# Decode attention: the rotary cache gathered with its features on the partitions, and the tied order of four transposes

## The chip, the cores and the metric

The kernel runs on one core of one Trainium2 chip. The metric is the device time of one execution in microseconds. The engines work side by side, each in the order of its own queue: PE (matrix products; its weight loads are shown as PEld), DVE (vector operations), ACT (scalar functions and copies), POOL (here it issues the gathers) and SP (here it issues the other loads and stores). A DMA queue moves data between the chip's memory (HBM) and the on-chip memory of 128 partitions.

## The reference, cut to what matters

One step of one layer: a feed-forward block, a mixer (a gated recurrence and a latent attention side by side), and a second feed-forward block, for a prompt of 512 tokens and 8 decoded sequences of 4 tokens each. The change is in the latent attention of the decoded sequences. Their past is 4096 tokens each, held in pages of 128 tokens that a page table names; a past token has a latent row of 256 numbers and a rotary row of 64:

```python
past_c = cache_kv_latent[l][page_table].reshape(Bs, past_len, KV_LORA)
past_r = cache_k_rope[l][page_table].reshape(Bs, past_len, QK_ROPE)
...
s = (jnp.einsum('bqhr,bsr->bhqs', ql, c_kv) + jnp.einsum('bqhd,bsd->bhqs', qr, k_rope)).astype(jnp.float32) * scale
s = jnp.where(k_pos[None, None, None, :] <= qp[None, None, :, None], s, -jnp.inf)
p = jax.nn.softmax(s, axis=-1).astype(c_kv.dtype)
return jnp.einsum('bhqs,bsr->bqhr', p, c_kv)
```

So a score is a sum over 256 + 64 features, and the value is taken from the latent rows alone. All in 32-bit floats.

## The kernel before, in words

The phases follow one another: first feed-forward block, mixer of the prompt, and then the decode (`decode`, L1437), which shares its time with the second feed-forward block of the prompt's first half (the generator `gb`). The loop at L1517 calls them in turn: a step of the decode, then about one step of the feed-forward block, of which there are 100 while the decode has 94.

The decode works on 16 halves: 8 sequences, 2048 past tokens at a time (`Half`, L1352). A half is two blocks of 1024 tokens. For a block POOL gathers the latent rows by an indirect DMA (`gather`, L1360: 128 partitions x 8 tokens x 256 features, 1 MB, into one of seven slots) and the rotary rows by another (`gather_r`, L1369: tile `rraw`, 128 x 8 x 64, 256 KB, two buffers). Both come with tokens on the partitions. A matmul needs the features there, so DVE turns the blocks by transposing squares of 32 x 32 (`turn`, L1376, the transposes of L1381): five stages per half, one of 64 features each, two transposes of 128 x 512 per stage. Stage 0 is the rotary one (`JS` = (8, 9) at L65), stages 1 to 4 the latent ones. The result of a stage is a tile `kh`, of which there are four buffers.

For scores (`score`, L1384) PE multiplies each stage with a query laid out in blocks of 64 x 32, eight small matmuls at a time for each of the two 32-feature groups; the products of all five stages add up in one bank. Then (end of `score`) ACT and DVE copy the scores out and DVE takes a row maximum (`self.top`, L1401). In `peak` (L1403) PE spreads the maximum, DVE reduces it (L1407) and takes the masked sum that serves as bias (L1410), ACT takes the exponential (L1411), DVE transposes the probabilities (L1413), and DVE and ACT place them into `pbuf` (L1417; four of the sixteen copies are DVE's). In `value` (L1419) PE multiplies them with the latent rows.

The halves are staggered. The outer loop counts n, with five steps st each. In an iteration half n-2 is scored (stages 0 to 2 at st 2, stages 3 and 4 at st 4, by `RUNS` at L68), half n-3 has its `peak` at st 1 and its values at st 4, after which its latent slots are gathered into again, and one stage is turned per step, in order of a list `ups`: at st 2 the last stage of half n-2, at st 3 and 4 stages 0 and 1 of half n-1, and at st 0 and 1 of the next iteration its stages 2 and 3. The rotary rows of a half are gathered as soon as the rotary stage of the half before has been turned.

Within an engine the order is not simply the order of the text: a planner lists the instructions by the text's order and its own reckoning of when each is ready, so a later one that is ready sooner may go first. `tc.issue_after(x)` ties what is traced under it behind x in the queue of x's engine; it adds no wait for x's end. Before the change one turn per iteration is tied, the one at st 4, behind `self.top`.

Of the kernel before, what the change touches and what calls it, by code (L numbers as in the profile page):

```python
# [73 lines left out]
C_W = C_SH + 2 * TS  # L74
# [4 lines left out]
def _constants():  # L79
    cf = np.zeros((P, C_W), np.float32)  # L80
    p = np.arange(P)
    cf[:, C_ID : C_ID + P] = np.eye(P, dtype=np.float32)
    pos = np.concatenate([np.arange(TP), PAST + np.tile(np.arange(NT), NB)]).astype(np.float32)
    half = RD // 2
    inv = np.power(np.float32(10000.0), -np.arange(half, dtype=np.float32) / np.float32(half)).astype(np.float32)
    ang = pos[None, :] * inv[p % half][:, None]
    cf[:, C_COS : C_COS + T] = np.cos(ang)
    cf[:, C_SIN : C_SIN + T] = np.sin(ang) * np.where(p % RD < half, -1.0, 1.0)[:, None]
    t = np.arange(T)
    cf[:, C_RST : C_RST + T] = np.where(t < TP, t % CH != 0, t % NT != 0)[None, :]  # L90
# [8 lines left out]
    cf[:, C_P8] = p % 16  # L99
    cf[:, C_S4 : C_S4 + 32] = p[:, None] % 32 == np.arange(32)[None, :]  # L100
# [10 lines left out]
def hybrid_step_kernel(  # L111
    ctx: ExitStack,
    tc: tile.TileContext,
    x_t, pool_c, pool_r, state, ptl, vecs, w_g, w_u, w_d, w_in, w_kr, w_q, w_qr, w_kv, w_uk, w_o, cf, cm,
# [656 lines left out]
    q2 = qsT.rearrange("p j b t h -> p j (b t h)")  # L771

# [16 lines left out]
    with scope("mix") as mx_:  # L789
# [293 lines left out]
        with scope("at2"):  # L1083
# [154 lines left out]
            def decode_prep():  # L1238
                for j in range(10):
# [62 lines left out]
    with scope("dec"):  # L1302
# [49 lines left out]
        class Half:  # L1352
            def __init__(self, n):
# [4 lines left out]
                self.craw, self.rraw, self.kh = [], [], []  # L1358
# [10 lines left out]
            def gather_r(self):  # L1369
                for blk in (2 * self.n, 2 * self.n + 1):  # L1370
                    rraw = mk([P, ROWS, RD], F32, "rraw", 2)
                    off = bass.IndirectOffsetOnAxis(ap=idx[:, blk : blk + 1], axis=0)
                    nc.gpsimd.indirect_dma_start(rraw.rearrange("p a r -> p (a r)"), None, pool_r, off)
# [10 lines left out]
            def score(self, st):  # L1384
# [3 lines left out]
                for jj, j in enumerate(JS[st]):  # L1388
                    for c in range(4):
                        for r in range(2):  # L1390
                            rs = slice(r * 64, r * 64 + 64)
                            kh = self.kh[st][rs, c // 2, c % 2 * 4 : c % 2 * 4 + 4, jj]
                            nc.tensor.matmul(self.s[r][c * 32 : c * 32 + 32, :P], q[rs, j], kh, start=st + jj == 0, stop=st == len(JS) - 1 and jj == 1, skip_group_check=True)  # L1393
# [9 lines left out]
            def peak(self):  # L1403
# [6 lines left out]
                nc.vector.scalar_tensor_tensor(mq, m, -SCALE, selL, op0=ALU.mult, op1=ALU.mult, accum_out=mb)  # L1410
# [3 lines left out]
                for c in range(4):  # L1414
                    for g in range(4):
                        src = pt[c * 32 : c * 32 + 32, g // 2 * 4 : g // 2 * 4 + 4, g % 2 * 16 : g % 2 * 16 + 16]
                        (nc.scalar.copy if g else nc.vector.tensor_copy)(self.p[g * 32 : g * 32 + 32, c // 2, c % 2 * 4 : c % 2 * 4 + 4, self.i * 16 : self.i * 16 + 16], src)  # L1417
# [19 lines left out]
        def decode():  # L1437
            H = [Half(n) for n in range(NH2)]
            blocks = [h_ for h_ in H for _ in range(2)]
            ups = [(h_, st) for h_ in H for st in range(len(JS))]  # L1440
# [6 lines left out]
            def turn(top):  # L1447
                if ups:
                    h_, st = ups.pop(0)
                    with tc.issue_after(top.ins) if top is not None else nullcontext():  # L1450
                        h_.turn(st)
                    if st == 0 and h_.n + 1 < NH2:
                        H[h_.n + 1].gather_r()

            for n in range(NH2 + 4):
# [4 lines left out]
                for st in range(len(JS)):  # L1460
                    if at(2):
                        for k in RUNS.get(st, ()):
                            at(2).score(k)
# [204 lines left out]
def _arrays(inputs):  # L1668
# [41 lines left out]
```

## Time and profile before

| | |
|---|---|
| time, median of 3 runs | 1250.94 us (1250.69 to 1252.57) |
| profiled execution, span from first to last instruction | 1241.4 us |
| what lies around the span, if the profiled execution was like the median (its own time is not given beyond the span) | 9.5 us |
| busy share of the span: PE, PEld, DVE, ACT, POOL | 98%, 93%, 79%, 60%, 6% |
| granted TensorE clock, mean | 0.999 |
| HBM traffic over the span | 156 GB/s |

The span is from the first to the last instruction of the program, the time includes what lies around it. An engine's busy time is the union of its instructions. Matmuls overlap, and their ends are modelled, so a busy PE is not PE at its peak. In a row of a timeline stand the start and the duration in microseconds, engine, line, operation, the tiles written and read, the shape, the count of merged instructions, and in brackets how long the engine had been idle and what ended that. In a row of waits stands who waited on whose result, in total, how many times, and the longest. Buffer numbers are left out of names, and a slot that several tiles use shows under one name (`q` is a large slot that also holds queries, scores and latent rows).

### The profile page before, as it was taken

The page shows a single profiled execution, that of the slowest core. Times are in us where ns is not written, and L with a number is a line of the kernel's source. Part 1 is how long each engine was busy: PE and PEld are TensorE (multiplying, and loading weights), DVE is VectorE, ACT ScalarE, POOL GpSimd, SP SyncE. Part 2 cuts the span into 40 slices and gives each one's busy share as a digit, 9 for nine tenths or more (in the row PEclk, how much of TensorE's full clock was granted, in tenths as well). Part 3 has the DMA queues.
Part 4 walks back from the last instruction along what each step waited for, and adds up shares of the span by engine and source line. Part 5 has one row for each costly group of instructions (what it writes and reads, how often), then busy time and mean ns, then how long its engine had stood idle before and what let it go on. Part 6 is the DMA issues. An engine that isn't in the chain of part 4 may idle for free.

```text
span 1241.4 us, 29997 instructions
## 1 busy us (share of the span) xinstructions
PE 1215.0 (98%) x12366; PEld 1151.3 (93%) x12366; DVE 982.7 (79%) x1976; ACT 738.8 (60%) x1559; POOL 76.5 (6%) x80
## 2 busy tenths in 40 slices
PE   8999999999999999999999999999999999999997
PEld 6999999999999989988898888888888999999997
DVE  7897788878678888786877899999998778566665
ACT  7675545455366744545758766666656776554455
POOL 0000000000000000000001312322310000000000
PEclk9999999999999999999999999999999999999999
DMA  6232333232264213333233868878776635545451
GB/s 238 86 115 90 103 103 102 86 99 91 62 221 147 82 54 105 88 94 130 85 105 117 339 214 303 310 282 323 258 275 232 198 106 188 184 137 188 150 151 60
DMA packets 73113, 195.59 MB, mean 158 GB/s; under 512 B 12336, under 2 KB 27728, under 8 KB 68240
## 3 DMA queue, kind: packets, MB, share of 16 engines
q1 hardware_dynamic: 64512, 150.47, 37.3%
q0 software_dynamic: 7168, 41.95, 9.2%
q8 instruction: 97, 1.59, 0.5%
q10 hardware_dynamic: 1296, 1.26, 0.3%
q14 instruction: 40, 0.33, 0.1%
HBM read 183.97 MB, written 9.67 MB: 156 GB/s over the span
## 4 chain that ended last, share of the span: by engine, by line
PE 79%; DVE 11%; ACT 7%; issue 2%; DMA 2%; SPq 0%; DVEq 0%; ACTq 0%
PE acc L259 29%; PE acc L277 13%; PE dn L259 8%; PE Y L575 7%; PE X L575 4%; PE Z L575 4%; DVE kh L1381 3%; PE acc L731 3%; DVE wl L251 2%; ACT wh L250 1%; PE s L1393 1%; ACT pbuf L1417 1%; DMA wraw<-w_g 1%; PE pa L952 1%; PE o L1426 1%
## 5 line engine op out<-in xcount | busy, mean ns | idle before, releaser
L250 ACT CAST wh<-wraw 128x1024 fp32r<-128x1024 f32 (+2 forms) x194 | 185.0, 957 | 164.3 <-PE acc L259 103.7
L251 DVE TENSOR_TENSOR wl<-wraw,wh 128x1024 fp32r<-128x1024 f32 (+2 forms) x194 | 214.6, 1108 | 72.2 <-ACT wh L250 71.6
L277 PE MATMUL acc<-uha,wh 128*128 128x256 f32 (+1 forms) x528 | 155.5, 295 | 0.1
L277 PE MATMUL acc<-uha,wl 128*128 128x256 f32 (+1 forms) x528 | 150.0, 285 | 0.8 <-DVE wl L251 0.7
L277 PE MATMUL acc<-ula,wh 128*128 128x256 f32 (+1 forms) x528 | 150.5, 286 | 0.0
L259 PE MATMUL acc<-uhb,wh 128*128 128x288 f32 (+1 forms) x432 | 128.0, 296 | 0.0
L259 PE MATMUL acc<-uhb,wl 128*128 128x288 f32 (+1 forms) x432 | 127.0, 295 | 1.0 <-DVE wl L251 0.8
L259 PE MATMUL acc<-ulb,wh 128*128 128x288 f32 (+1 forms) x432 | 127.5, 295 | 0.0
L277 PEld LDWEIGHTS acc<-uha,wh 128*128 128x128 f32 x528 | 99.2, 188 | 8.8 <-issue 7.9
L277 PEld LDWEIGHTS acc<-uha,wl 128*128 128x128 f32 x528 | 99.2, 188 | 2.3 <-DVE wl L251 1.6
L277 PEld LDWEIGHTS acc<-ula,wh 128*128 128x128 f32 x528 | 99.4, 188 | 1.6 <-issue 1.2
L259 PEld LDWEIGHTS acc<-uhb,wl 128*128 128x128 f32 x432 | 81.2, 188 | 1.6 <-DVE wl L251 1.6
L259 PEld LDWEIGHTS acc<-uhb,wh 128*128 128x128 f32 x432 | 81.0, 187 | 0.2 <-ACT uhb L170 0.2
L259 PEld LDWEIGHTS acc<-ulb,wh 128*128 128x128 f32 x432 | 81.1, 188 | 0.1
L259 PE MATMUL dn<-hh,dh 128*128 128x272 f32 x256 | 74.3, 290 | 0.0
L259 PE MATMUL dn<-hh,dl 128*128 128x272 f32 x256 | 73.7, 288 | 0.0
L259 PE MATMUL dn<-hl,dh 128*128 128x272 f32 x256 | 73.6, 288 | 0.0
L277 PE MATMUL acc<-uhb,wh 128*128 128x272 f32 x176 | 52.8, 300 | 0.0
L1417 ACT COPY pbuf<-pt 32x64 f32<-32x64 f32 x192 | 46.5, 242 | 10.1 <-DVE pt L1413 7.3
L259 PE MATMUL acc<-hlb,wh 128*128 128x288 f32 x176 | 52.1, 298 | 0.0
L259 PE MATMUL acc<-hhb,wh 128*128 128x288 f32 x176 | 51.8, 298 | 0.0
L1393 PE MATMUL s<-kh,q 64*32 64x128 f32 x2560 | 48.0, 273 | 3.5 <-DVE kh L1381 3.5
(632 smaller groups left out, 3881.3 us busy)
## 6 DMA issues: line engine op xcount, KB each, us to landing
wraw<-w_u SPq DMA_DIRECT2D x66, 512.0 KB, 4.3
wraw<-w_g SPq DMA_DIRECT2D x65, 512.0 KB, 3.9
wraw<-w_d SPq DMA_DIRECT2D x40, 384.0 KB, 3.5
wraw<-w_in SPq DMA_DIRECT2D x24, 512.0 KB, 3.5
wraw<-w_d SPq DMA_DIRECT2D x32, 320.0 KB, 3.1
wraw<-w_d SPq DMA_DIRECT2D x16, 512.0 KB, 3.8
wraw<-w_o SPq DMA_DIRECT2D x16, 512.0 KB, 3.7
g_S<-state SPq DMA_DIRECT2D x4, 512.0 KB, 4.4
```

What stands on the lines that cost most here:

```text
L250: nc.scalar.copy(wh[:, :kt], w[:, :kt])
L251: nc.vector.tensor_tensor(wl[:, :kt], w[:, :kt], f32(wh[:, :kt]), op=ALU.subtract)
L259: nc.tensor.matmul(out, a, b, start=n == 0, stop=n == last)
L277: nc.tensor.matmul(acc[:, :n], a[:, k], b[:, k], start=k + i == 0, stop=k == kt - 1 and i == 2)
L575: nc.tensor.matmul(bank, a[p][:, k], b[q][:, k], start=first and k + n == 0, stop=k == 3 and n == 2, skip_group_check=True)
L731: nc.tensor.matmul(accs[x, d], wts[d][p][:, k], hs[k // 2][q][:, k % 2, x], start=k + n == 0, stop=k == nf - 1 and n == 2)
L952: nc.tensor.matmul(po[es, c].rearrange("p (n m) -> p n m", m=m), kx[:, cs], up(qx[:, cs], m), start=True, stop=True, skip_group_check=True)
L1381: nc.vector.transpose(kh[:, g].rearrange("p a j k -> p a (j k)"), src)
L1393: nc.tensor.matmul(self.s[r][c * 32 : c * 32 + 32, :P], q[rs, j], kh, start=st + jj == 0, stop=st == len(JS) - 1 and jj == 1, skip_group_c ...
L1417: (nc.scalar.copy if g else nc.vector.tensor_copy)(self.p[g * 32 : g * 32 + 32, c // 2, c % 2 * 4 : c % 2 * 4 + 4, self.i * 16 : self.i * ...
L1426: nc.tensor.matmul(o[g : g + 32, :R], self.p[:, c, a], self.craw[c][:, a], start=i + c == 0 and a < 4, stop=i + c == 2 and a >= 4, skip_gr ...
```

## The change

The rotary cache is laid out differently on the host, before the kernel starts: within a page first the number of a feature in its group of 32, then the group (two), then a token's place among eight, then sixteen. A gathered row is now 1 KB and holds one feature of each group for all 128 tokens of a page; before it was 2 KB and held 64 features of eight tokens. A second index (`idr`, 64 columns instead of 32), made in `decode_prep` from a page table of its own, names these rows, and `gather_r` makes four gathers of 128 KB per half into tiles `rk` instead of two of 256 KB into `rraw`. They arrive with features on the partitions: the rotary stage needs no transposes any more, and PE reads `rk` directly.

The rotary gathers of a half are issued at st 3, when the half before has had its rotary stage scored. The four remaining stages are turned at other steps: stages 1 and 2 of half n-1 at st 3 and st 4, stages 3 and 4 of half n-2 at st 1, one tied behind the masked sum of `peak`, the other behind DVE's last placed copy. The order of the scores is as before, with the rotary stage first.

```diff
             def decode_prep():
+                pr_sb = mk([P, 2 * NBLK], I32, "pr_sb")
+                nc.sync.dma_start(pr_sb, ptr)
+                p32 = mk([P, 1], F32, "p32")
+                nc.sync.dma_start(p32, cf[:, C_P32 : C_P32 + 1])
+                nc.vector.tensor_scalar(out=idr, in0=pr_sb, scalar1=float(RD // 2), scalar2=p32, op0=ALU.mult, op1=ALU.add)
...
             def gather_r(self):
                 for blk in (2 * self.n, 2 * self.n + 1):
-                    rraw = mk([P, ROWS, RD], F32, "rraw", 2)
-                    off = bass.IndirectOffsetOnAxis(ap=idx[:, blk : blk + 1], axis=0)
-                    nc.gpsimd.indirect_dma_start(rraw.rearrange("p a r -> p (a r)"), None, pool_r, off)
-                    self.rraw.append(rraw)
+                    rk = mk([P, 2, 2, ROWS, 16], F32, "rk", 2)
+                    for i in range(2):
+                        off = bass.IndirectOffsetOnAxis(ap=idr[:, 2 * blk + i : 2 * blk + i + 1], axis=0)
+                        nc.gpsimd.indirect_dma_start(rk[:, i].rearrange("p j a k -> p (j a k)"), None, pool_r, off)
+                    self.rk.append(rk)
...
-                    src = self.craw[g][:, :, j * 32 : j * 32 + 64] if j < 8 else self.rraw[g]
+                    src = self.craw[g][:, :, j * 32 : j * 32 + 64]
...
-                            rs = slice(r * 64, r * 64 + 64)
-                            kh = self.kh[st][rs, c // 2, c % 2 * 4 : c % 2 * 4 + 4, jj]
-                            nc.tensor.matmul(self.s[r][c * 32 : c * 32 + 32, :P], q[rs, j], kh, start=st + jj == 0, stop=st == len(JS) - 1 and jj == 1, skip_group_check=True)
+                            rs, as_ = slice(r * 64, r * 64 + 64), slice(c % 2 * 4, c % 2 * 4 + 4)
+                            out = self.s[r][c * 32 : c * 32 + 32, :P]
+                            if j < 8:
+                                kh = self.kh[st - 1][rs, c // 2, as_, jj]
+                            else:
+                                kh = self.rk[c // 2][rs, :, jj, as_].rearrange("p i a k -> p a i k")
+                                out = out.rearrange("p (a i k) -> p a i k", a=4, i=2)
+                            nc.tensor.matmul(out, q[rs, j], kh, start=st + jj == 0, stop=st == len(JS) - 1 and jj == 1, skip_group_check=True)
...
-                nc.vector.scalar_tensor_tensor(mq, m, -SCALE, selL, op0=ALU.mult, op1=ALU.mult, accum_out=mb)
+                self.spread = nc.vector.scalar_tensor_tensor(mq, m, -SCALE, selL, op0=ALU.mult, op1=ALU.mult, accum_out=mb)
...
+                        if g == 0:
+                            self.placed = put
...
-            ups = [(h_, st) for h_ in H for st in range(len(JS))]
+            ups = [(h_, st) for h_ in H for st in range(1, len(JS))]
...
-            def turn(top):
+            def turn(after=None):
                 if ups:
                     h_, st = ups.pop(0)
-                    with tc.issue_after(top.ins) if top is not None else nullcontext():
+                    with tc.issue_after(after.ins) if after is not None else nullcontext():
                         h_.turn(st)
-                    if st == 0 and h_.n + 1 < NH2:
-                        H[h_.n + 1].gather_r()
...
-                        if n == 0:
-                            H[0].gather_r()
                         gather(2 + n // 2)
+                    if st == 3 and at(1):
+                        at(1).gather_r()
...
-                    if n > 1 or n == 1 and st >= 1:
-                        if n != 2 or st >= 2:
-                            turn(at(2).top if at(2) and st == len(JS) - 1 else None)
+                    if n > 0 and st > 2:
+                        turn(at(2).top if at(2) and st == len(JS) - 1 else None)
+                    if n > 1 and st == 1:
+                        turn(at(3) and at(3).spread)
+                        turn(at(3) and at(3).placed)
...
-        "pool_r": g["cache_k_rope"].reshape(-1, ROWS * RD),
+        "pool_r": np.ascontiguousarray(g["cache_k_rope"].reshape(-1, 16, ROWS, 2, 32).transpose(0, 4, 3, 2, 1)).reshape(-1, 16 * ROWS * 2),
+        "ptr": np.ascontiguousarray(np.repeat(g["page_table"].reshape(NBLK, 4, 2), 32, axis=1).transpose(1, 0, 2)).reshape(P, 2 * NBLK),
```

More of the change, by code (lines that the diff above doesn't have):

```diff
@@ L73 @@
 C_SH = C_SL + 16
-C_W = C_SH + 2 * TS
+C_P32 = C_SH + 2 * TS
+C_W = C_P32 + 1
 V_QG, V_KVG, V_HGG, V_LB = 48, 54, 56, 57
@@ L113, in hybrid_step_kernel @@
     tc: tile.TileContext,
-    x_t, pool_c, pool_r, state, ptl, vecs, w_g, w_u, w_d, w_in, w_kr, w_q, w_qr, w_kv, w_uk, w_o, cf, cm,
+    x_t, pool_c, pool_r, state, ptl, ptr, vecs, w_g, w_u, w_d, w_in, w_kr, w_q, w_qr, w_kv, w_uk, w_o, cf, cm,
     y_a, y_p, y_s, ckv_p, kr_p, st_p, ckv_s, kr_s, st_s,
@@ L1357, in __init__ @@
                 self.e = dq[:, 0, 640 + n % 2 * 256 : 896 + n % 2 * 256]
-                self.craw, self.rraw, self.kh = [], [], []
+                self.craw, self.rk, self.kh = [], [], []
             def gather(self):
@@ L1416, in peak @@
                         src = pt[c * 32 : c * 32 + 32, g // 2 * 4 : g // 2 * 4 + 4, g % 2 * 16 : g % 2 * 16 + 16]
[L1417 removed]
+                        put = (nc.scalar.copy if g else nc.vector.tensor_copy)(self.p[g * 32 : g * 32 + 32, c // 2, c % 2 * 4 : c % 2 * 4 + 4, self.i * 16 : self.i * 16 + 16], src)
+                        if g == 0:
+                            self.placed = put
             def value(self, mate, c):
@@ L1460, in decode @@
                 for st in range(len(JS)):
-                    if at(2):
-                        for k in RUNS.get(st, ()):
-                            at(2).score(k)
+                    for k in RUNS.get(st, ()) if at(2) else ():
+                        at(2).score(k)
                     if n < 3 and st == 0:
-                        if n == 0:
-                            H[0].gather_r()
                         gather(2 + n // 2)
+                    if st == 3 and at(1):
+                        at(1).gather_r()
                     if st == PEAK and at(3):
```

2 lines of the change are left out of this document (added).

## The prediction

> **What bounds the kernel now.** I read the page first, then the stretch in which the diff works (the decode), then who waits there, then one period of it instruction by instruction.
>
> ```profile
> span 1241.4 us, 29997 instructions
> PE 1215.0 (98%) x12366; PEld 1151.3 (93%) x12366; DVE 982.7 (79%) x1976; ACT 738.8 (60%) x1559; POOL 76.5 (6%) x80
> ```
>
> Over the span PE is the bound. The next view is the decode stretch alone, 697 to 945 us: all engines.
>
> ```profile
> core 0: us, PE busy (x) PEld busy (x) DVE busy (x) ACT busy (x) POOL busy (x), PEclk, DMA share, GB/s
> 697.00:945.00 248.00, 243.48 (x4409) 214.92 (x4409) 233.64 (x508) 155.84 (x406) 64.06 (x58) 1.00 0.78 278
> ```
>
> And DVE's time in line 1381 by itself:
>
> ```profile
> 697.00:945.00 248.00, 100.63 (x160) 1.00 0.78 278
> ```
>
> Two engines are nearly full: PE 243.5 of 248 us and DVE 233.6 (94%), 100.6 us of it in the 160 transposes of line 1381. The gain can only be the time in which PE stands for DVE, so the waits of its weight loads decide (window 690 to 945 us; us in total, times, longest):
>
> ```profile
> PEld s L1393 <- DVE kh L1381: 5.4, 7, 1.7
> ...
> PEld acc L277 <- DVE wl L251: 1.6, 3, 1.0
> ```
>
> I price PE's waits with the loads' rows, since a matmul is drawn to its modelled end and hides the start of a wait: 5.4 us lost to late transposes, in 7 places, 1.6 us to late weight splits. That is all that PE loses to DVE: 7.0 us of 248. One period shows how such a wait comes about. First PE, then DVE.
>
> ```profile
> 792.94 1.59 PE L1393 MATMUL s<-kh,q 64*32 64x128 f32 x96
> ...
> 803.40 0.38 PE L1405 MATMUL pm<-ident,mxh 128*128 128x128 f32 x2
> ...
> 805.13 1.59 PE L1393 MATMUL s<-kh,q 64*32 64x128 f32 x96
> ...
> 809.69 0.87 PE L1393 MATMUL s<-kh,q 64*32 64x128 f32 x40
> 810.84 0.64 PE L1393 MATMUL s<-kh,q 64*32 64x128 f32 x24 [0.28 <-DVE kh L1381]
> ...
> 818.40 1.59 PE L1393 MATMUL s<-kh,q 64*32 64x128 f32 x96
> ```
>
> ```profile
> 805.17 0.67 DVE L1381 STREAM_TRANSPOSE kh<-dx 128x512 f32<-128x512 f32 x1
> ...
> 806.14 0.42 DVE L365 TENSOR_TENSOR sil<-sil,acc 128x256 f32<-128x256 f32 x1
> 806.48 0.28 DVE L1407 TENSOR_REDUCE q<-pm 128x16 f32<-128x128 f32 x1
> 806.79 0.17 DVE L1410 SCALAR_TENSOR_TENSOR mq<-q 128x16 f32<-128x16 f32 x1
> 806.89 1.22 DVE L251 TENSOR_TENSOR wl<-wraw,wh 128x1024 fp32r<-128x1024 f32 x1
> 808.03 0.41 DVE L171 TENSOR_TENSOR hla<-sil,hha 128x256 fp32r<-128x256 f32 x1
> 808.37 0.43 DVE L1413 STREAM_TRANSPOSE pt<-q 128x256 f32<-128x256 f32 x1
> 808.73 0.67 DVE L1381 STREAM_TRANSPOSE kh<-q 128x512 f32<-128x512 f32 x1
> 809.32 0.74 DVE L1417 COPY pbuf<-pt 32x64 f32<-32x64 f32 x4
> 810.07 0.71 DVE L1381 STREAM_TRANSPOSE kh<-dx 128x512 f32<-128x512 f32 x1
> 810.71 1.26 DVE L1381 STREAM_TRANSPOSE kh<-rraw 128x512 f32<-128x512 f32 x2
> ```
>
> The maximum's broadcast (L1405) is on PE at 803.40, but DVE is in transposes until 805.84 and takes it up at 806.48, 2.7 us after its end (the column of durations is the second). The last latent transpose, which the run of scores at 809.69 needs after 40 of its 64 records (0.56 us, at (1.59 - 0.27)/95 = 13.9 ns a record), at 810.25, ends at 810.78: PE stands. Right behind it come two rotary transposes for the next half.
>
> **The change part by part.** *Removed:* the rotary transposes, 32 of line 1381's 160, by the row
>
> ```profile
> L1381 DVE STREAM_TRANSPOSE kh<-rraw x32: 668/670/712, 707.3 to 924.8; 128x512 f32<-128x512 f32 x32
> ```
>
> In steady state two start 0.63 us apart (1.26 for both), so with the overlap 32 cost 20 us (100.63 x 32/160 = 20.1). DVE falls from 94% to 86% of the stretch. On PE this is worth only the waits it ends. *Moved:* per half, stages 1 and 2 now run at steps 3 and 4, stages 3 and 4 at step 1, behind the masked sum (L1410) and the last placed copy (L1417). Between the broadcast's end (803.8) and the need for stage 4 (810.2) lie 6.4 us. The tied chain is 0.28 + 0.17 (the reduce and the sum), 1.3 (stage 3), 0.43, 0.74, 1.3 (stage 4) = 4.2 us; the exponential on ACT runs beside stage 3. If the planner puts all of L365, wl and hla (0.42 + 1.22 + 0.41) between, it is 6.25: in time, by nothing. Without them 2 us to spare. Seen the other way, in this period DVE has two transposes less ahead of stage 4 (1.3 us) and was 0.53 us late. The longest wait of the 7 is 1.7 us; I leave 0.35 us in two of them: 5.4 - 0.7 = **4.7 us gained**. Bounds: none (the chain ends late by what it was late before) and 5.4.
>
> The weight splits (1.6 us in 3 waits) stand behind the same transposes: I take half, **0.8 us gained** (bounds 0 and 1.6).
>
> *Added, on PE:* a half's scores now wait for four rotary landings themselves, where one DVE wait stood. What such waits cost the loads' sequencer shows the row of the value matmuls, which read landed tiles already (ns, minimum, median, maximum):
>
> ```profile
> L1426 PEldq EVENT_SEMAPHORE  x36: 51/51/1212, 739.2 to 950.2; - x36
> ```
>
> Four exposed in 16 halves are 3.3 us, none exposed is 0; the sequencer runs ahead of the array, so I take one: 16 x 0.051 = **0.8 us lost**. The rotary scores read runs of 16 elements instead of 32, in an order of three strides. The nearest rows are matmuls over a moving operand with gaps and one without:
>
> ```profile
> 435.48 1.12 PE L952 MATMUL pa<-g_E 128*64 128x32 f32 x32
> ```
>
> ```profile
> 441.86 0.68 PE L954 MATMUL pa<-g_q,g_k 128*64 128x64 f32 x15
> ```
>
> Less the 0.22 us that the last one takes, 29 ns for 32 columns with gaps and 33 ns for 64 without. Both look like a floor for small ones, so this bounds badly: from no cost to 1.76 times per column, which on a fifth of the scores (160 records a half by the rows above, so 0.2 x 160 x 16 x 13.9 ns = 7.1 us) is 5.4 us. The old tile was read with gaps too (every second run of 32 in its row), which is nearer: I take 0.
>
> *Added, on POOL and the DMA queues:* four gathers of 128 KB per half for two of 256 KB, 32 issues more. Their rows (issue in ns, landing in us; minimum, median, maximum), and the queue's on the page (packets, MB, share of 16 engines):
>
> ```profile
> L1373 POOL DMA_INDIRECT rraw<-pool_r,idx x32: 947/954/1998, 690.1 to 912.0; - x32
> DMA to landing us min/median/max: 3.3/4.7/9.8
> ```
>
> ```profile
> q0 software_dynamic: 7168, 41.95, 9.2%
> ```
>
> At 0.95 us and a gap of 0.3 (as between POOL's other issues, an estimate), 32 issues are 40 us on an engine that is busy 64 of 248. Queued behind a rotary gather that waits on POOL are only the latent gathers of the same iteration, which wait for a later value matmul anyhow; they no longer stand behind rotary issues that wait for DVE. The bytes stay, in rows of 1 KB instead of 2. A packet of this queue took 0.092 x 16 x 1241.4/7168 = 0.255 us; if each of the 4096 rows that are added cost one, the 16 DMA engines would have 65 us more in 248, from a share of 0.78 to 1.04; if time goes by bytes, nothing. The packets held 5.9 KB each, more than the rows' mean of 5.1 (41.95 MB in 8192 rows), so rows are already sent together: I take nothing. On the path: 0, as long as they land in time (below); the other end is priced there. [...]
>
> *Added, once:* two small loads on SP and one DVE operation in the attention. The same operation and load for the latent index are
>
> ```profile
> L550 DVE TENSOR_SCALAR ptf<-ptf,p x1: 233/233/233, 32.7 to 32.7; 128x32 f32<-128x32 f32 x1
> ```
>
> ```profile
> DMA to landing us min/median/max: 8.2/8.2/8.2
> ```
>
> **0.2 us lost**; if DVE stood for the whole landing in front of the attention's work, 8.2. SP issues weights several tiles ahead, so the load should long be there when DVE comes to it; only the weights behind it on SP wait, for two issues.
>
> **Sum:** -4.7 - 0.8 + 0.8 + 0.2 = -4.5 us on the profiled span of 1241.4, so 1236.9. What lies around the span is 1250.94 - 1241.4 = 9.5 us if the profiled execution was like the median (only its span is given), which gives **1246.4 us**. About 0.2%, 2.5 us, is what a measurement of this kernel can tell from no change.
>
> **The rivals.** *No change: the wait moves.* The tied chain cannot start stage 4 before ACT's exponential, the sheet transpose and four copies; with 2 us of feed-forward work in between it ends when it is needed, and in halves where ACT or the broadcast is late PE stands as before. For it: 6.25 against 6.4 us. Against: 20 us of DVE work is gone, so the reduce should no longer be 2.7 us late. Left of the gain about 1 us, less 1 us of added waits: 1250.9 us.
>
> *Slower: the rotary keys land late.* Their buffers come free only when stage 0 of the half before has been scored, 0.44 us into a run of 96 (32 records). Three issues of 1.25 us later, at 4.2 us, the fourth starts; the next run stands 12.2 us after the last one in the shortest halves (792.94 to 805.13), 13.3 in the next (to 818.40). So 8.0 us are left in the shortest. The median landing of 4.7 fits with 3.3 us to spare, the longest of 9.8 does not: 1.8 us late there, 0.7 in halves of 13.3. If such landings were the rule and half of the halves like these two (an estimate), 8 would lose 1.25 us on average, 10 us, PE standing in order behind the rotary scores: 1250.9 - 4.5 + 10 = 1256.4 us. It decides from landings of some 8.5 us or issues that all take 2 us (then 3.1 us later, spare used up). Now the transposes take the landing long before PE needs it; that cover goes. Against: smaller gathers, issued when the latent ones have mostly landed. [...]
>
> *More: all waits of the stretch go* and none come: 7.0 us, 1243.9.
>
> **How the numbers follow.** Forecast (with partial gains of over 2.5 us) 0.50, more 0.08, no change 0.25, slower 0.17. So faster 0.58, same 0.25, slower 0.17. The forecast's own range is 1243.9 to 1248.4. The range for 8 in 10 takes in the first three and the milder part of a late landing or a dear access pattern: 1242.8 to 1253.5.
>
> **What would show it.** Right: line 1381 with 128 transposes and about 80 us; DVE near 86% of the stretch; PE's waits on kh under 1 us; L1407 within 1 us of L1405's end; no wait of PE for the rotary tile. Wrong: kh still ahead in PE's waits with the copies of L1417 just before it (no change); a wait of the scores for the rotary landing, or the first fifth of each run of 96 drawn out (slower); DVE standing before its new index operation in the attention.

## The result and the profile after

The changed kernel takes 1332.4 us (median of six runs, 1327.2 to 1341.3) where the kernel before takes 1250.5 (1248.2 to 1252.6): a ratio of 1.066, with an interval of 1.063 to 1.069. It is 82 us slower; 4.5 us less was predicted.

The page of the changed kernel, span, engines and the row of the granted clock:

```profile
span 1325.4 us, 30033 instructions
...
PE 1267.6 (96%) x12366; PEld 1183.1 (89%) x12366; DVE 970.3 (73%) x1945; ACT 739.5 (56%) x1559; POOL 104.5 (8%) x112
...
PEclk9999999999999999999999898788989999999999
```

The new digits 7 and 8 lie in the decode. The waits of the weight loads from 690 to 1040 us (total, times, longest), the scores being line 1407 now, tell what PE stands for there (it stands when it starts no instruction):

```profile
PEld s L1407 <- issue: 55.9, 91, 1.3
PEld acc L279 <- issue: 8.6, 23, 0.5
```

The 5.4 us that waited for turned keys (before: line 1393 on DVE's kh) have gone. In their place are 55.9 us that the profile puts on "issue": the engine waited for no semaphore and no data that is recorded. One half, first PE, then POOL:

```profile
869.30 0.67 PE L1407 MATMUL s<-rk,q 64*32 64x128 f32 x32
869.76 0.91 PE L1407 MATMUL s<-kh,q 64*32 64x128 f32 x44
870.85 0.39 PE L1407 MATMUL s<-kh,q 64*32 64x128 f32 x3 [0.17 <-issue]
871.60 0.42 PE L1407 MATMUL s<-kh,q 64*32 64x128 f32 x3 [0.37 <-issue]
872.37 0.39 PE L1407 MATMUL s<-kh,q 64*32 64x128 f32 x3 [0.34 <-issue]
873.12 0.42 PE L1407 MATMUL s<-kh,q 64*32 64x128 f32 x3 [0.36 <-issue]
873.86 0.37 PE L1407 MATMUL s<-kh,q 64*32 64x128 f32 x1 [0.32 <-issue]
874.60 0.43 PE L1407 MATMUL s<-kh,q 64*32 64x128 f32 x2 [0.38 <-issue]
876.01 0.65 PE L1407 MATMUL s<-kh,q 64*32 64x128 f32 x5 [0.98 <-issue]
```

```profile
870.25 0.95 POOL L1382 DMA_INDIRECT rk<-pool_r,idr  x1 [3.91 <-PE s L1407]
871.50 0.95 POOL L1382 DMA_INDIRECT rk<-pool_r,idr  x1 [0.30 <-issue]
872.76 0.95 POOL L1382 DMA_INDIRECT rk<-pool_r,idr  x1 [0.30 <-issue]
874.01 0.95 POOL L1382 DMA_INDIRECT rk<-pool_r,idr  x1 [0.30 <-issue]
```

The run begins at its old pace; the 32 rotary matmuls, with their new access pattern, take no longer than others (the next group starts 0.46 us later). After 76 of 96 it comes to a stand and goes on in groups of one to five, some 0.7 us apart, until it has lasted 7.3 us instead of 1.5. The stands begin where POOL issues the four gathers of the next half, which the last rotary matmul has just released, 0.95 us behind the run's start; the last stand outlasts the fourth issue by 1 us. In that last microsecond no other engine is busy, and PE hardly (PE, PEld, DVE, ACT, POOL; then granted clock, DMA share, GB/s):

```profile
875.00:876.00 1.00, 0.03 (x2) 0.12 (x1) 0.00 (x0) 0.00 (x0) 0.00 (x0) 0.50 0.36 98
```

The windows of this half (PE, PEld, DVE, ACT, POOL busy; granted clock; DMA share; GB/s), with the whole stretch on top:

```profile
697.00:1029.00 332.00, 296.07 (x4417) 246.20 (x4418) 222.06 (x476) 156.76 (x406) 89.73 (x88) 0.90 0.61 209
866.00:870.00 4.00, 4.00 (x80) 3.87 (x81) 3.16 (x8) 3.10 (x7) 0.34 (x1) 1.00 0.84 315
870.00:874.00 4.00, 2.44 (x57) 1.03 (x40) 2.87 (x9) 3.60 (x14) 2.85 (x3) 0.94 0.92 342
874.00:878.00 4.00, 2.64 (x14) 1.88 (x14) 1.95 (x4) 0.02 (x1) 0.95 (x1) 0.50 0.28 82
878.00:882.00 4.00, 4.00 (x72) 3.86 (x76) 0.96 (x2) 0.73 (x1) 0.00 (x0) 0.71 0.33 98
882.00:886.00 4.00, 4.00 (x79) 2.88 (x63) 3.21 (x6) 1.87 (x6) 1.89 (x2) 1.00 0.43 127
```

So there is a second cost. In windows of 1 us the granted clock is 0.50 from 874 to 880 us and 1.00 again from 881, some 4 us behind the last stand; the feed-forward matmuls in between start 0.21 us apart instead of 0.12. The spans of the two profiles differ by 84.0 us. Added up from the records, the runs of scores last 111.4 us in all, where they last 50.1 in the profile before: 61.3 more, although the 5.4 us of waits have gone. The clock is at 0.50 for 64.9 us of the decode, 20.2 of them inside these runs; the other 44.6 are worth up to 22.3 us (an estimate: half of that time if the pace falls with the clock; the matmuls above start 0.21 us apart for 0.12). Together that is 83.6.

### The profile page after: what moved, and what is told of

It reads as the page before. It is cut to its first block, busy times and chain, and to the rows that moved or that the text cites. A ratio compares the mean times of both kernels' runs of the same rounds, so it can differ in the third digit from the quotient of the medians.

```text
span 1325.4 us, 30033 instructions
## 1 busy us (share of the span) xinstructions
PE 1267.6 (96%) x12366; PEld 1183.1 (89%) x12366; DVE 970.3 (73%) x1945; ACT 739.5 (56%) x1559; POOL 104.5 (8%) x112
## 4 chain that ended last, share of the span: by engine, by line
PE 90%; ACT 4%; issue 3%; DVE 3%; DMA 0%; DVEq 0%; SPq 0%; ACTq 0%
PE acc L261 29%; PE acc L279 20%; PE dn L261 7%; PE Y L577 6%; PE s L1407 6%; PE X L577 4%; PE Z L577 4%; PE acc L733 3%; PE o L1442 2%; PE pa L955 1%; PE acc L290 1%; ACT wh L252 1%; PE s L1205 1%; PE o L1237 1%; PE zx L843 1%
## 5 line engine op out<-in xcount | busy, mean ns | idle before, releaser
L279 PE MATMUL acc<-uha,wh 128*128 128x256 f32 (+1 forms) x528 | 162.9, 309 | 0.4 <-issue 0.4
L279 PE MATMUL acc<-ula,wh 128*128 128x256 f32 (+1 forms) x528 | 157.9, 300 | 0.1
L279 PE MATMUL acc<-uha,wl 128*128 128x256 f32 (+1 forms) x528 | 156.9, 298 | 0.1
L279 PEld LDWEIGHTS acc<-uha,wh 128*128 128x128 f32 x528 | 107.2, 203 | 9.8 <-issue 9.0
L279 PEld LDWEIGHTS acc<-ula,wh 128*128 128x128 f32 x528 | 107.1, 203 | 2.4 <-issue 2.0
L279 PEld LDWEIGHTS acc<-uha,wl 128*128 128x128 f32 x528 | 106.8, 202 | 1.3 <-issue 0.7
L1407 PE MATMUL s<-kh,q 64*32 64x128 f32 x2048 | 71.0, 278 | 34.5 <-issue 34.1
L1407 PEld LDWEIGHTS s<-kh,q 64*32 64x32 f32 x2048 | 41.0, 106 | 58.2 <-issue 55.9
L1382 POOL DMA_INDIRECT rk<-pool_r,idr x64 | 65.1, 1017 | 109.7 <-PE s L1407 86.4
```

Of the source, the lines that this page charges most:

```text
L279: nc.tensor.matmul(acc[:, :n], a[:, k], b[:, k], start=k + i == 0, stop=k == kt - 1 and i == 2)
L1382: nc.gpsimd.indirect_dma_start(rk[:, i].rearrange("p j a k -> p (j a k)"), None, pool_r, off)
L1407: nc.tensor.matmul(out, q[rs, j], kh, start=st + jj == 0, stop=st == len(JS) - 1 and jj == 1, skip_group_check=True)
```

## The experiments

The runs went to different chips. On some the kernel before takes 1243.5 to 1245.1 us, on the others, that of the result among them, 1250.3 to 1250.5; I call them the 1244 chips and the 1250 chips. A ratio is always against the kernel before on the same chip. e1 to e8 fell on 1244 chips, before it was known that this matters.

The page of the kernel before belongs to the 1244 kind. Its span is 1241.4 us; in all other runs, the changed kernel's among them, the time is 1.7 to 1.8 us more than the span, so that execution took about 1243.2 us. No profile shows the kernel before on a 1250 chip.

### e1_mid and e14_mid: the same change, the gathers released behind the run

```diff
-JS = ((8, 9), (0, 1), (2, 3), (4, 5), (6, 7))
+JS = ((0, 1), (2, 3), (8, 9), (4, 5), (6, 7))
```

(and the numbering of the latent stages with it.)

> The changed kernel with the rotary stage scored third instead of first, so it ends the run of 96 matmuls instead of beginning it; the buffers of the rotary keys come free at that run's end, and POOL issues the next half's four gathers behind the run and not inside it. Issue theory (POOL's issuing of indirect gathers slows the feeding of TensorE, which a long run of 14 ns matmuls feels): every run of 96 takes about 1.3 us again, granted clock back to 1.00, 1242 to 1252 us; if the feed-forward matmuls behind the run feel the issues as well, up to 1275. Layout rival (reading the rotary keys in their new layout, or their new rows, is what costs): the runs stay broken, 1325 to 1340. Order rival (the tied order of the turned stages costs): 1325 to 1340, since that order stays.

On a 1244 chip: 1241.0 us against 1244.0, ratio 0.9971 (0.9961 to 0.9981), the runs of 96 whole (no stand in them). I took this for proof of the issue theory; it was not yet, as no control of the changed kernel had run on such a chip. On a 1250 chip, beside that control:

> e1_mid (rotary stage third, its gathers released at the end of the run of 96) beside the control on the same chip. On a 1250 chip its issues, which fall between the runs, meet the run of 64 behind them in most halves (in e1_mid two issues, from 0.3 us before it on); in the changed kernel's profile a run of 64 with two issues at such a place took 2.6 us instead of 0.89, so up to 12 x 1.7 = 20 us and some for the clock: 1250 to 1280. On a 1244 chip 0.9971 again. If the release point were not the cause, the control's time.

1274.5 us, 1.0196 (1.0177 to 1.0215), where the control (e13) has 1.0682. The runs of 96 are whole. The stands are in the runs of 64 behind them, which POOL's last one or two rotary issues meet (waits of the loads, then one such run on PE, then POOL):

```profile
PEld s L1407 <- issue: 26.5, 35, 1.3
```

```profile
806.43 0.66 PE L1407 MATMUL s<-kh,q 64*32 64x128 f32 x30
807.93 0.44 PE L1407 MATMUL s<-kh,q 64*32 64x128 f32 x4 [0.84 <-issue]
808.70 0.45 PE L1407 MATMUL s<-kh,q 64*32 64x128 f32 x8 [0.33 <-issue]
809.46 0.69 PE L1407 MATMUL s<-kh,q 64*32 64x128 f32 x22 [0.30 <-issue]
```

```profile
806.13 0.95 POOL L1382 DMA_INDIRECT rk<-pool_r,idr  x1 [0.30 <-issue]
807.38 2.00 POOL L1382 DMA_INDIRECT rk<-pool_r,idr  x1 [0.30 <-issue]
```

Moving the rotary stage, and the release with it, takes away 60 of the 84 us there, and the stands move with the issues.

### e2_dummy, e5_dummy_early and e16_dummy_early: the issues alone, in the kernel before

```diff
+            def extra(self):
+                self.dm = mk([P, 4, 16], F32, "dm")
+                for i in range(4):
+                    off = bass.IndirectOffsetOnAxis(ap=idx[:, 2 * self.n + i // 2 : 2 * self.n + i // 2 + 1], axis=0)
+                    nc.gpsimd.indirect_dma_start(self.dm[:, i], None, pool_r.rearrange("n (i c) -> (n i) c", c=16), off)
...
+                    if st == 0 and jj == 1 and hasattr(self, "dm"):
+                        for i in range(4):
+                            nc.tensor.matmul(self.s[0][:32, P + 16 * i : P + 16 * i + 16], q[:64, 8], self.dm[:64, i], start=True, stop=True, skip_group_check=True)
...
+                    if st == 3 and at(1):
+                        at(1).extra()
```

In e2 the extra matmuls stand behind stage 0 instead.

> The kernel before (old layout, old order, transposed rotary keys), with four more indirect gathers per half of 64 bytes a row, released as in the changed kernel by the first stage of the half before it; four small extra matmuls per half read them, into columns that nobody uses. Nothing of the computation is left out. Issue theory: the runs of 96 break after some 75 records into small groups as in the changed kernel and take 5 to 7 us, 1310 to 1340 us. Rivals of layout, order and of the transfer's data (8 KB a gather is next to nothing): the runs stay at 1.3 us, 1249 to 1256 us (60 small matmuls and 60 issues that nobody waits for).

Unlike that text says, something is left out: the extra matmuls have `start=True` in the bank of the scores, and by the author's reckoning one quarter of the old pages' scores is not the reference's for it. On a 1244 chip 1250.7 us, ratio 1.005 (1.003 to 1.0069), the runs not broken: a miss for the issue theory. The first extra issue fell 1.18 us behind the run's start, when most of it was through; so the readers were moved forward:

> The kernel before with the same four extra gathers of 64 bytes a row as e2, but their readers stand in the middle of the first stage of the run, so that POOL's first extra issue falls some 0.9 us behind the run's start (as in the changed kernel, 0.94) and not 1.18. The extra matmuls open an accumulation in the bank of the scores, so one quarter of the old pages' scores is not that of the reference (as in e2). Issue theory: runs of 104 records broken after some 75 to 85, 5 to 7 us long, time 5 to 7% over the kernel before. Size rival (it takes the 1 KB rows of the rotary gathers, not their issue): runs whole as in e2, time within 0.7% of the kernel before.

On a 1244 chip 1250.2 us, 1.0035 (1.0023 to 1.0048). A run with an issue inside it lost some 0.3 us, 0.4 at most: a miss again. The same kernel on a 1250 chip:

> e5 (the kernel before with four extra gathers of 64 bytes a row, issued from 0.96 us behind the start of the run on; the old pages' scores of one quarter differ, as there) beside the control. Issue theory on a 1250 chip: broken like the control, since only the issues are new: 5 to 7 us a run, 5 to 8% over the kernel before. If the cause is in the changed kernel (layout, order, bytes), within 0.7% of the kernel before there as well. On a 1244 chip as e5, 1.0035.

1342.1 us, 1.0727 (1.0704 to 1.075), more than the changed kernel loses there. The same run of 104 in e5 (1244 chip) and then in e16 (1250 chip):

```profile
823.04 0.45 PE L1402 MATMUL s<-kh,q 64*32 64x128 f32 x16
...
823.50 1.79 PE L1402 MATMUL s<-kh,q 64*32 64x128 f32 x76
825.22 0.39 PE L277 MATMUL acc<-uha,wh 128*128 128x256 f32 x1
```

```profile
822.10 0.45 PE L1402 MATMUL s<-kh,q 64*32 64x128 f32 x16
...
822.57 0.93 PE L1402 MATMUL s<-kh,q 64*32 64x128 f32 x43
823.65 0.44 PE L1402 MATMUL s<-kh,q 64*32 64x128 f32 x5 [0.15 <-issue]
824.42 0.39 PE L1402 MATMUL s<-kh,q 64*32 64x128 f32 x3 [0.34 <-issue]
...
828.78 0.62 PE L1402 MATMUL s<-kh,q 64*32 64x128 f32 x18 [0.44 <-issue]
829.32 0.51 PE L277 MATMUL acc<-uha,wh 128*128 128x256 f32 x1
```

2.2 us on the one chip, 7.2 on the other, with POOL's issues 0.96 us behind the run's start and 0.95 us long on both (the first at 824.00 and at 823.07). This kernel has the old layout, the old order, and 8 KB a gather more: so the four issues a half, with the small matmuls that read them, make the loss without any other part of the change. How large it is went with the chip. Each chip was used at one time only, so chip and time are not told apart; the pair e1 and e14 agrees.

### e9_control and e13_control: the changed kernel beside the others

> The changed kernel itself, as it is, beside the runs that follow: e5 and e6 lost 0.3 to 0.4 us at the first issue inside a run of 96, where the changed kernel's own profile lost 0.5 us there and 4 to 5 behind it. If that is the kernel's property, 6 to 7% over the kernel before again, runs of 5.3 to 6.9 us. If it was of that execution or chip, about e6's time (within 1.5% of the kernel before) and runs of 1.7 to 3.

> The changed kernel again, as the control of this call. e1 to e8 ran on chips on which the kernel before takes 1244 to 1245 us, e9 to e12 and the first timing on chips on which it takes 1250. On a 1250 chip: 6 to 7% over the kernel before, runs of 5.3 to 6.9 us. On a 1244 chip the issue theory as e5 and e6 leave it (0.3 to 0.6 us lost at an issue) says runs of 1.7 to 2.2 us and between 0 and 1.5% over; if the chips don't differ, 6 to 7% over there too.

Both fell on 1250 chips: 1331.8 us, 1.0658 (1.0635 to 1.0681), and 1334.1, 1.0682 (1.0652 to 1.0711). The result repeats on 1250 chips. On a 1244 chip the changed kernel itself was never timed.

### e6_two, e10_idx and e11_half: how many issues, and which

```diff
-                    for i in range(2):
-                        off = bass.IndirectOffsetOnAxis(ap=idr[:, 2 * blk + i : 2 * blk + i + 1], axis=0)
-                        nc.gpsimd.indirect_dma_start(rk[:, i].rearrange("p j a k -> p (j a k)"), None, pool_r, off)
+                    off = bass.IndirectOffsetOnAxis(ap=idr[:, 2 * blk : 2 * blk + 1], axis=0)
+                    nc.gpsimd.indirect_dma_start(rk[:, 0].rearrange("p j a k -> p (j a k)"), None, pool_r, off)
+                    r0 = (2 * blk + 1) * P
+                    nc.sync.dma_start(rk[:, 1].rearrange("p j a k -> p (j a k)"), pool_r[r0 : r0 + P])
```

That is e11. e10 only reads `idx[:, blk : blk + 1]` in place of the `idr` columns; e6 issues one gather of 2 KB rows through `idx` in place of the two.

> The changed kernel with the rotary keys of a half brought by two gathers of 2 KB rows and not four of 1 KB, same bytes, same release; the rows hold other pages' keys in part, so the old pages' rotary scores are not those of the reference. In the changed kernel's own profile a run of 96 lasts 1.9 us with one issue inside, 3.2 with two and 5.3 to 6.9 with four. Issue theory: two inside, so runs of about 3.2 us, 15 x 1.9 = 28 us over e1_mid and some for the clock: 1 to 3.5% over the kernel before. Data rival: as the changed kernel, 6 to 7% over it.

On a 1244 chip: 1245.7 us, 1.000 (0.9988 to 1.0012), runs of about 1.9 us, over before the second issue. Below the range.

> The changed kernel with its four gathers of 1 KB rows reading the latent pages' index tile and not the new one (other rows, so the old pages' rotary scores are of other keys). Four issues as in the changed kernel. If four issues behind each other hold the run, broken as in e9. If the new index tile or the neighbouring rows that it names do it, runs of about 1.7 us, 1240 to 1255.

On a 1250 chip 1327.7 us (one execution), broken like the control: the index tile and the rows it names don't matter.

> The changed kernel with two of a half's four gathers (1 KB rows, the new index tile) and the other two replaced by plain loads on SP of consecutive rows (so some of the old pages' rotary keys are others). If the 1 KB rows hold the run, it stands 0.5 us at the first issue as in the changed kernel and ends behind the second, 2.5 to 3.5 us, 1265 to 1290; if it is the number of issues behind each other, 1.7 us as in e6, 1240 to 1255.

On the same chip 1282.4 us (one execution) against 1250.4 and the control's 1331.8. The run holds at the first issue and ends behind the second:

```profile
819.93 0.67 PE L1408 MATMUL s<-rk,q 64*32 64x128 f32 x32
820.39 0.89 PE L1408 MATMUL s<-kh,q 64*32 64x128 f32 x43
821.45 0.31 PE L1408 MATMUL s<-kh,q 64*32 64x128 f32 x2 [0.17 <-issue]
...
823.71 0.52 PE L1408 MATMUL s<-kh,q 64*32 64x128 f32 x13 [0.36 <-issue]
824.16 0.39 PE L279 MATMUL acc<-uha,wh 128*128 128x256 f32 x1
```

4.2 us with two issues, 7.3 with four: on average about 1.4 us for each over the 1.5 of a whole run, and 32 us lost instead of 81. The bytes that came at that moment were the same. The average hides a spread: the two runs of 96 in the changed kernel's profile that meet one issue alone, a longer one of 1.84 and 1.41 us (runs at 734.41 and 771.51 us), last 2.1 us, 0.6 over a whole run.

### e3_sp, e18_sp, e4_memset and e7_plain: the same moment without gathers

```diff
-                        off = bass.IndirectOffsetOnAxis(ap=idr[:, 2 * blk + i : 2 * blk + i + 1], axis=0)
-                        nc.gpsimd.indirect_dma_start(rk[:, i].rearrange("p j a k -> p (j a k)"), None, pool_r, off)
+                        r0 = (2 * blk + i) * P
+                        nc.sync.dma_start(rk[:, i].rearrange("p j a k -> p (j a k)"), pool_r[r0 : r0 + P])
```

e7 has `nc.gpsimd.dma_start` there, e4 three times `nc.gpsimd.memset(rk[:, i], ...)`.

> The changed kernel with the rotary keys brought by plain loads on SP's queue, as many, of the same bytes, into the same tiles and released by the same matmuls; they bring consecutive rows and not the rows of the page table, so the old pages' rotary scores are of other keys. Issue theory: runs of 96 whole (1.3 us), 1240 to 1255 us, perhaps up to 1265 if the weights queued on SP behind a load that waits come late. Data rival (the rotary keys' transfers at that moment slow TensorE): broken as before, 1310 to 1340.

> The changed kernel with the rotary tiles written by POOL memsets (three for each gather, so POOL is busy for several us at the same place) instead of gathers; the old pages' rotary keys are constants. Issue theory (it is the issuing of gathers): runs of 96 whole, 1238 to 1252 us. Rival (POOL being busy at all at that place, whatever it does): broken, over 1300.

> The changed kernel with the rotary keys brought by four plain loads per half that POOL issues, same bytes, same release and place; consecutive rows and not those of the page table, so the old pages' rotary scores are of other keys. If it is the indirect gather's issue (0.95 us each, POOL working out 128 rows): runs whole, 1238 to 1255 us. If any issue of a transfer by POOL at that place does it: broken, over 1290.

> e3 again (rotary keys by plain loads on SP, same bytes, tiles and release, consecutive rows instead of the page table's), timed. On a 1250 chip: the issue theory says that the change without its extra gathers gives what the prediction summed, 0.1 to 0.6% under the kernel before, every run of 96 whole; the data rival says broken runs, 2 to 7% over. On a 1244 chip about 0.997, as e3's single time.

All four fell on 1244 chips. In one execution each, e3 takes 1240.8 us (the kernel before 1244.0), e4 1237.5 (1244.0) and e7 1239.4 (1245.1); e18, the median of eleven, takes 1242.6 against 1243.5, 0.9987 (0.9979 to 0.9996). No run of 96 is broken; the gain of e18 is smaller than expected. But on these chips a gather hardly costs either, so against the rivals they say little; that a plain load or a memset by POOL is free on a 1250 chip was not tried. Against the data rival stand e11 and e16.

### e8_untied: the ties

This is e1's kernel without the ties:

```diff
-                        turn(at(2).top if at(2) and st == len(JS) - 1 else None)
+                        turn()
...
-                        turn(at(3) and at(3).spread)
-                        turn(at(3) and at(3).placed)
+                        turn()
+                        turn()
```

> e1_mid without the three ties: the turned latent stages stand at the same steps, but not behind the maximum, the masked sum and the placed copy. Nothing is left out. If the ties are worth the waits that the prediction gave them (4.7 us), 1 to 5 us slower than e1_mid, with waits of TensorE for turned keys; if only the 32 transposes less count, within 1 us of it. The runs of 96 are whole either way.

1241.0 us, 0.9967 (0.9954 to 0.9979) on a 1244 chip, as e1, and no wait for turned keys either. The ties are worth nothing that can be measured; that there are 32 transposes less, and four places for the others, is enough.

### e12_split: a shorter first run

```diff
-RUNS = {2: (0, 1, 2), 4: (3, 4)}
+RUNS = {2: (0, 1), 3: (2,), 4: (3, 4)}
```

> The changed kernel with the run of 96 cut: the rotary stage and the first latent one at step 2 (64 matmuls), the second latent one at step 3 (32), feed-forward matmuls between; the gathers are still issued 0.94 us behind the run's start, when 64 matmuls are through (0.9 us). Nothing is left out. Issue theory: no run meets an issue for long, every run whole, about e1_mid's time, 0.2 to 0.5% under the kernel before. If the issues slow TensorE at that place whatever runs there, still over 1290.

On a 1250 chip 1309.7 us, 1.0461 (1.0444 to 1.0479): a miss. The run of 64 is whole, since the first issue comes when it is through. But 2.7 us behind its start the 32 others meet the second issue and those behind it:

```profile
807.25 0.67 PE L1407 MATMUL s<-rk,q 64*32 64x128 f32 x32
807.72 0.72 PE L1407 MATMUL s<-kh,q 64*32 64x128 f32 x32
809.99 0.70 PE L1407 MATMUL s<-kh,q 64*32 64x128 f32 x9
811.05 0.31 PE L1407 MATMUL s<-kh,q 64*32 64x128 f32 x2 [0.35 <-issue]
...
813.91 0.79 PE L1407 MATMUL s<-kh,q 64*32 64x128 f32 x17 [1.02 <-issue]
```

They stop after 9 matmuls and last 4.7 us (their share of a whole run is 0.45). It isn't the length of a run that counts, as I had written, but that small matmuls and issues fall together.

### e15_late and e17_late2: all issues out of the runs

```diff
-JS = ((8, 9), (0, 1), (2, 3), (4, 5), (6, 7))
-RUNS = {2: (0, 1, 2), 4: (3, 4)}
+JS = ((0, 1), (2, 3), (4, 5), (6, 7), (8, 9))
+RUNS = {2: (0, 1), 4: (2, 3, 4)}
...
-                    if st == 3 and at(1):
+                    if st == 4 and at(1):
                         at(1).gather_r()
```

> The rotary stage scored last of all (JS in the order of the latent stages, then rotary; runs of 64 and then of 96), the next half's rotary gathers issued behind the run of 96 at step 4, before the latent ones. All issues of a half then stand in the 8 us between the run of 96 and the next run of 64. Issue theory: no run meets more than the end of one issue, on either kind of chip 0.1 to 0.6% under the kernel before; if the last issue runs into the run of 64, up to 1% over it on a 1250 chip.

On a 1250 chip 1273.5 us, 1.0171 (1.0141 to 1.0202), above the range. All six issues of a half stand between the run of 96 and the next of 64, but the last of them runs into it, or ends less than 0.2 us ahead of it, in about half of the halves:

```profile
820.11 0.66 PE L1407 MATMUL s<-kh,q 64*32 64x128 f32 x31
821.80 0.77 PE L1407 MATMUL s<-kh,q 64*32 64x128 f32 x33 [1.03 <-issue]
```

The other runs are whole, but for waits for turned keys (3.7 us in six places) and a few places where they are a little longer. The feed-forward matmuls, beside which most issues stand here, lose as well: stands on "issue" of 18.5 us in lines 261, 279 and 290, where the profile before has 9.5 (6.7, 2.0 and 0.8). e17 moves one latent gather away:

```diff
-                        for c in range(2):
-                            at(3).value(at(4), c)
-                            gather()
+                        at(3).value(at(4), 0)
+                        gather()
...
+                    if st == 2 and at(4):
+                        at(4).value(at(5), 1)
+                        gather()
+                    if st == 3 and at(4) and at(4).i:
+                        at(4).gathered()
```

> e15_late with the second value block of each half (and with it one of the half's two latent gathers, which its end releases) moved behind the next run of 64 at step 2, and the gathered outputs of a pair from step 1 to step 3. Five issues (6.3 us) then stand between the run of 96 and the run of 64 (8.2 us and more in e15), one behind the run of 64. Nothing is left out. Issue theory: on a 1250 chip no run meets an issue, 0.1 to 0.6% under the kernel before; if the feed-forward matmuls feel the issues there (30 stands of 10 us in all in e15's profile), up to 0.8% over it. On a 1244 chip about 0.997.

It fell on a 1244 chip: 1259.1 us, 1.0136 (1.0112 to 1.016), a miss, most of it with a cause of its own. The matmuls of `gathered` now stand one step behind the copy that they read:

```profile
PEld o L1450 <- ACT q L1445: 12.9, 8, 3.0
```

So whether the loss goes entirely on a 1250 chip stays open, and no kernel of these beats the kernel before there. e1 and e8 do on 1244 chips, by 0.3%.

## Why the prediction was wrong

**The removed waits: right.** The 128 transposes that are left take 83.7 us in the changed kernel (80 forecast). The wait for turned keys is gone in it and in e1: 5.4 us, where 4.7 were taken. In e1, whose decode fills the same 247 us, DVE is busy for 218.3, 88% (86 forecast), and the reduce of the broadcast follows its end by 0.5 to 0.9 us in three halves (under 1 forecast). The chain behind it ends in time, so the rival "the wait moves" falls.

**The weight splits: not there.** In e1 PE still waits for them as before, up to 1040 us:

```profile
PEld acc L279 <- DVE wl L253: 1.7, 2, 1.4
PEld acc L261 <- DVE wl L253: 1.6, 3, 0.8
```

The first line is the wait that the prediction priced, 1.7 us where it was 1.6. The second lies behind the decode's stretch, at line 261, which is line 259 of the kernel before, where it was the same:

```profile
PEld acc L259 <- DVE wl L251: 1.6, 3, 0.8
```

So the 0.8 us are no gain.

**The waits of the rotary scores: small, as forecast.** The prediction has the loads' sequencer run ahead of the array; in the profile before, 33 of the 36 waits in its row of L1426 were over while the load ahead of them was still under way, by 4 to 57 ns. The landing is no wait of PE in any profile with gathers, and the rotary matmuls' access pattern costs nothing (the next group starts 0.46 us behind them, where the prediction had 0.44). In e1, which moves the rotary stage and is only near to the forecast kernel, the 5.4 us are gone, one stand of 0.9 us has come, and the 15 runs of 96 are 1.1 us longer in all than in the profile before. Its ratio is 2.4 to 4.9 us off 1244; the forecast of -4.5 lies in that.

**The 9.5 us around the span: not there.** They are 1.8 in every run that has both numbers. The page before came from an execution of about 1243.2 us and not from one like the median. This lowers the level of the forecast, and leaves the change that it forecasts.

**The step that failed** is the part on POOL: "On the path: 0, as long as they land in time". It counted the 32 added issues as 40 us on an idle engine, and asked only when their data come. The issues had the forecast size, 0.95 us each and 0.30 between (median 0.947 us, where it was 0.954), and PE stands, not POOL; the first came 0.95 us behind the run's start, and not at 0.44. What was missing is that PE stands at POOL's issues: e16 shows it without the layout and the order of the change, e14 moves the place and the stands go with it, e11 halves the issues and the stands. On 1250 chips that is on average about 1.4 us for each of four issues in a run of scores, where the prediction has 0, and the half clock behind the stands comes on top. In the kernel before, the rotary tile came free behind DVE's transposes, and no run of 96 met an issue; the release at the rotary stage's end puts up to four of them into it. Why PE stands there, and why on these chips only, stays open. The slower rival named that release, but a different price: landings 1.8 us late. And the sign that it set, the first fifth of the run drawn out, was the wrong end: the last fifth is. That a slower time was given 0.17 says nothing for the prediction, since no rival of it has PE stand at an issue.

## What to carry to other kernels

An engine that nobody waits for can still hold another one (here a run of scores lasted 7.3 us instead of 1.5 beside four of POOL's issues): before a release point is moved, look at what runs on TensorE while the work that it releases is issued, not only at whether the data come in time. Keep POOL's gathers beside large matmuls, which felt them far less here (in e15, 9 us more of stands for some 90 issues, about 0.1 us each by this estimate), and away from runs of small ones. Time a change on more than one chip before its experiments are read: the same kernel is 0.4% over the kernel before on one (e5) and 7% on another (e16).

## What the runs showed of the hardware that was not expected

On some chips a row of POOL's issues of indirect gathers holds back a stream of small matmuls that has all its data: from 13.9 ns a matmul to about three in 0.7 us, 7.2 us for the run of 104 in e16. On others the same kernel loses 0.3 us at the same place (2.2 us for that run in e5). It isn't the bytes (64 a row suffice, e16), the index tile (e10 takes 1327.7 us without it) or DVE, which has no busy time from 873 to 876 us while PE stands. No run separates POOL's work on an issue from the transfer that it sets off. What holds PE was not shown: the profile has no wait there. That its instructions come too late was the author's guess; no run shows it, and the instruction packets speak against it. Queue q8, of the kind instruction on the page, has 97 packets of 16 KB, about one for every 128 of the 12366 matmuls with their loads, so they are taken as PE's instructions (an estimate from that count). In 67 of the 91 stands of the loads in line 1407 (55.9 us in all) none of them was under way; and the matmuls come in groups of one to five, not by the 128. What differs between the chips is open too. The 6.6 us by which the kernel before is slower on 1250 chips may be the same effect, since its runs of 64 meet issues as well; no run shows it.
